# Two partial sums of a convolution block added up later, and a state-space branch that starts each of three parts one step later

## The chip, the cores and the metric

The kernel runs on one core of a Trainium2 chip. Its engines are TensorE (PE, matrix products), VectorE (DVE), ScalarE (ACT) and GpSimd (POOL); each takes its instructions in the order in which the program lists them. GpSimd also issues most of the smaller transfers, SyncE those of the weights. The metric is the device time of one execution in microseconds (us); less is better.

## The reference

Two blocks are computed on 512 tokens of width 1024, in float32. The first is an attention block with a gated feed-forward layer. The second is a mixer of two branches and a mixture of experts. The change is in the mixer, of which this matters:

```python
u = u_a * sigmoid(u_b)                                   # glu
u = silu(layernorm(causal_dwconv(u, cv_dw_w) + cv_dw_b)) # 31 taps per channel
y_cv = u @ w_cv_out
xbc = silu(causal_dwconv(xbc))                           # 4 taps
xs, bm, cm = split(xbc); dt = softplus(...)
y = ssd(xs, dt, a, bm, cm) + d_skip * xs                 # state space, 4 groups
y = rmsnorm_per_group(y * silu(z)); y_ssm = y @ w_ssm_out
return (g_cv * y_cv + g_ssm * y_ssm) @ w_mix_out
```

## The kernel before, in words

Activations lie with channels on the 128 partitions and the 512 tokens along the free axis. Every large product of the mixer is made from three float32r products (high part by high part, and the two mixed ones), `mm3` at L185 to L187. Weights come in through a stream: SyncE loads a raw tile, ACT makes its high part (L80) and DVE its low part (L81), two tiles ahead of their use.

`mixer` runs one list of product stages in a fixed order, `u0 p0 z0 u1 p1 w0 z1 u2 p2 w1 z2 u3 p3 w2 z3 c0 w3`, and then the second half of the gates. A stage `u` makes two blocks of the convolution branch (128 channels each), `p` the inputs of one of four state-space groups, `z` the gates of that group, `w` the group's part of the output product, `c` half of the gates of the convolution branch. Each stage is cut into steps of twelve products of 128x512 and then one call of `tick`; a stage `u`, `z` or `w` has 8 steps, `p` has 12, `c` has 16. Below, u1.7 is the seventh step of stage u1. A tick does not order the work in time by itself: it decides where in each engine's queue the instructions of the side work stand.

Three kinds of side work hang on the ticks:

- `conv31(m, pad, i)`, the 31 taps of block m. Blocks with an even m (`i == 0`) run on DVE, one instruction per tap (L1235). Blocks with an odd m (`i == 1`) are added up by transfers: ACT scales the shifted input into a tile `tap` (L1240), and POOL issues a transfer that adds it to one of two partial sums (L1241), the even taps to `acc`, the odd ones to `two[1]`. After the last tap DVE adds the two sums (L1244), POOL writes the result out to `ucd` (L1245) and adds it to `S1`, the sum over the blocks (L1246). A rate per stage says how many taps go into one tick.
- `ssd(g)`, the state-space group g, a generator that moves one step per tick (every second tick in a stage `w`). Its steps are in order: the products of B and C (L1324), four turns of the inputs (`xtr`, L1339 on PE, L1341 on DVE, L1345 on POOL), the chunk states (`state`, L1352), four pairs of decay matrices (`seg`, L1367 to L1378, their product on DVE at L1372), four outputs (`out`, L1387 and L1391 on PE into one bank psC, emptied by DVE at L1394), a column sum for the norm (L1467 on PE, fed by POOL at L1404), an inverse root on POOL (L144 to L151), diagonal matrices on POOL (L1457), their product (L1461), and the normalized rows `yh`, `yl` (L1449 and L263 on DVE, L262 on ACT). Stage `w` of the group multiplies these rows.
- `ln`, the layer norm of the convolution branch. It waits in its generator until all `conv31` are through, loads the eight blocks again, makes the mean from `S1` (L1530), subtracts it (L1537 on DVE, L1539 on ACT, L1543 on POOL), forms a column sum (L1467 again) and scales.

`WAIT` holds three digits for each group g. `ssd` passes over so many steps before its first products, before its column sum, and (in `rstd_row`) between the inverse root and the diagonal matrices.

After the mixer comes the mixture of experts. Which expert weights it loads is computed from the mixer's output, all but those of its first unit.

Of the kernel before, what the change touches and what calls it, by code (L numbers as in the profile page):

```python
# [13 lines left out]
OP = mybir.AluOpType  # L14
# [1098 lines left out]

WAIT = "000 000 000 000".split()

NTAP = 4  # L1120


def mixer(K, a):
# [6 lines left out]
    v_, s_, p_ = nc.vector, nc.scalar, nc.gpsimd  # L1130
# [89 lines left out]
    ucd = K.dr.tile([8, 128, S], F32, name="ucd")  # L1220
    S1 = g_()
    p_.memset(S1, 0.0)

    def conv31(m, pad, i):
        acc = g_()
        if i == 0:
            v_.tensor_scalar(acc, pad[:, 0:S], K.cw31[:, m, 0:1], K.cols[:, m:m + 1], op0=OP.mult, op1=OP.add)
        else:

            two = (acc, g_())  # L1230
            s_.activation(acc, pad[:, 0:S], AF.Identity, scale=K.cw31[:, m, 0:1], bias=K.cols[:, m:m + 1])
        yield 1
        for k in range(1, 31):
            if i == 0:
                v_.scalar_tensor_tensor(acc, pad[:, k:k + S], K.cw31[:, m, k:k + 1], acc, op0=OP.mult, op1=OP.add)  # L1235
            elif k == 1:
                s_.activation(two[1], pad[:, k:k + S], AF.Copy, scale=K.cw31[:, m, k:k + 1])
            else:
                t = gp.tile([128, S], F32, name="tap", tag="tap", bufs=NTAP)
                s_.activation(t, pad[:, k:k + S], AF.Copy, scale=K.cw31[:, m, k:k + 1])  # L1240
                p_.dma_start(two[k % 2], t, accum_op=OP.add)  # L1241
            yield 1
        if i:
            v_.tensor_tensor(acc, acc, two[1], op=OP.add)  # L1244
        p_.dma_start(ucd[m], acc)  # L1245
        p_.tensor_tensor(S1, S1, acc, op=OP.add)  # L1246

    hold = {}

    def evac_u(q, e, acc):  # L1250
        if e < 2:
            hold[2 * q + e] = acc
            return
        m = 2 * q + e - 2
        th = g_()
        s_.activation(th, acc, AF.Tanh, scale=0.5)
        pad = pad_(30, 4)
        p_.memset(pad[:, 0:30], 0.0)
        v_.scalar_tensor_tensor(pad[:, 30:], th, 1.0, hold.pop(m), op0=OP.add, op1=OP.mult)
        i = m % 2  # L1260
        bg[i].append(conv31(m, pad, i))
# [40 lines left out]
    def pause(n):  # L1302
        for _ in range(n):
            yield

    def ssd(g):
        d = gr[g]
        while not all(i in d for i in range(6)):
            yield
        wait = [int(n) for n in WAIT[g]]  # L1310
        yield from pause(wait[0])
# [207 lines left out]
    def ln():  # L1519
        while bg[0] or bg[1]:  # L1520
            yield
        for m in range(8):
            u = pad_(30, 4) if m < 4 else pad_(3, 3) if m < 7 else gp.tile([128, S], F32, name="tap", tag="tap", bufs=NTAP)
            p_.dma_start(u[:, 0:S], ucd[m])
# [835 lines left out]
def fused_kernel(ctx: ExitStack, tc: tile.TileContext, a, out, dbg=None, stage=9):  # L2360
# [60 lines left out]
    with tc.tile_pool(name="big3", bufs=1) as K.big:  # L2421
        K.ng = 38
        K.taps = {'u': (1.5, 1.5, 1), 'p': (0.1, 0.8, 1), 'z': (2, 1.25, 1), 'w': (1.5, 1, 0.5), 'c': (2.5, 0.25, 1)}
        mixer(K, a)
# [55 lines left out]
```

## Time and profile before

| | |
|---|---|
| time of three runs, median (lowest to highest) | 2449.02 us (2448.45 to 2449.63) |
| the profiled execution: time, span | 2449.14 us, 2447.3 us |
| mean granted TensorE clock, as a share of full speed | 0.986 |
| TensorE busy | 2255.6 us, 92% of the span |
| DVE, ACT, POOL busy | 51%, 33%, 18% of the span |

The span reaches from the first to the last instruction. The mixer's stages lie between about 780 and 1440 us of it. Since matrix products are pipelined, an engine that is busy is not one at its peak; what stands idle before an instruction, and what ended that idle time, is the more telling number.

### The profile page before, as it was taken

How to read it: one execution, taken by the hardware profiler on the slowest of the kernel's cores; microseconds unless marked ns; L12 is line 12 of the kernel's file. 1: busy time of each engine (PE TensorE's matmuls, PEld its weight loads, DVE VectorE, ACT ScalarE, POOL GpSimd, SP SyncE). 2: the span in 40 equal slices, each digit the busy share in tenths (PEclk: the TensorE clock that was granted, in tenths of full speed). 3: DMA queues.
4: the chain of work that ended last, by engine and by line, in shares of the span. 5: the costliest groups of instructions: out<-in, count | busy, mean ns of one | idle time of the engine just before them, and what ended most of it. 6: DMA issues, size and time to landing. Idle time of an engine off the chain costs nothing.

```text
span 2447.3 us, 32777 instructions
## 1 busy us (share of the span) xinstructions
PE 2255.6 (92%) x12323; PEld 1524.1 (62%) x12323; DVE 1259.7 (51%) x2217; ACT 816.9 (33%) x1527; POOL 440.7 (18%) x746
## 2 busy tenths in 40 slices
PE   8999999999999999999999998989889888987775
PEld 6678878878888777787877785434334333433331
DVE  4456656763336677787875646434334334332222
ACT  5455654222225746465653533101001000100002
POOL 2044422230001243334334020000000000000001
PEclk9999999999999999999999999999999999999998
DMA  4121127865323666566653357999999999999996
GB/s 141 54 68 36 53 95 257 277 204 113 101 97 96 153 129 155 125 151 139 158 130 121 109 206 289 426 426 426 427 426 427 426 427 426 427 426 427 427 426 270
DMA packets 197521, 593.28 MB, mean 242 GB/s; under 512 B 16515, under 2 KB 104703, under 8 KB 148720
## 3 DMA queue, kind: packets, MB, share of 16 engines
q1 hardware_dynamic: 168016, 523.94, 55.0%
q0 software_dynamic: 29344, 67.22, 12.4%
q8 instruction: 98, 1.61, 0.2%
q14 instruction: 63, 0.52, 0.1%
HBM read 556.40 MB, written 4.22 MB: 229 GB/s over the span
## 4 chain that ended last, share of the span: by engine, by line
PE 55%; DMA 28%; DVE 8%; ACT 4%; issue 2%; POOL 2%; SPq 0%; ACTq 0%; POOLq 0%; DVEq 0%
DMA we<-in_w_dram 26%; PE psA L185 11%; PE psA L187 11%; PE psA L186 11%; PE psA L2132 3%; PE psA L2148 2%; PE psB L2065 2%; DMA g<-tap 2%; PE psE L185 1%; PE psE L186 1%; PE psE L187 1%; DVE w_l L81 1%; PE psC L765 1%; ACT w_h L80 1%; PE psB L739 1%
## 5 line engine op out<-in xcount | busy, mean ns | idle before, releaser
L81 DVE TENSOR_TENSOR w_l<-w_raw,w_h 128x1024 fp32r<-128x1024 f32 (+1 forms) x224 | 278.3, 1246 | 303.9 <-ACT w_h L80 303.3
L2132 PE MATMUL psA<-we,xe 128*32 128x512 f32 (+1 forms) x2048 | 352.3, 614 | 59.6 <-DMA we<-in_w_dram 58.7
L185 PE MATMUL psA<-xh,w_h 128*128 128x512 f32 (+1 forms) x960 | 379.7, 396 | 0.8 <-ACT w_h L80 0.8
L187 PE MATMUL psA<-xh,w_l 128*128 128x512 f32 (+1 forms) x960 | 368.6, 384 | 0.5 <-DVE w_l L81 0.5
L186 PE MATMUL psA<-xl,w_h 128*128 128x512 f32 (+1 forms) x960 | 368.1, 383 | 0.7 <-DVE xl L263 0.7
L80 ACT CAST w_h<-w_raw 128x1024 fp32r<-128x1024 f32 (+1 forms) x224 | 232.8, 1043 | 236.4 <-PE psA L187 113.7
L2132 PEld LDWEIGHTS psA<-we,xe 128*32 128x32 f32 (+1 forms) x2048 | 88.4, 119 | 275.5 <-issue 169.4
L2148 PE MATMUL psA<-we,t 128*32 128x512 f32 (+1 forms) x1024 | 188.8, 619 | 38.2 <-DMA we<-in_w_dram 37.5
L185 PEld LDWEIGHTS psA<-xh,w_h 128*128 128x128 f32 x960 | 181.4, 189 | 41.1 <-issue 4.9
L186 PEld LDWEIGHTS psA<-xl,w_h 128*128 128x128 f32 x960 | 181.4, 189 | 39.1 <-issue 4.6
L187 PEld LDWEIGHTS psA<-xh,w_l 128*128 128x128 f32 x960 | 181.0, 189 | 37.5 <-DVE w_l L81 1.0
L2114 DVE TENSOR_TENSOR res<-res,psC 128x512 f32<-128x512 f32 x78 | 53.5, 686 | 267.9 <-PE psC L2112 267.8
L2053 POOL TENSOR_TENSOR ow<-ow,owb 128x128 f32<-128x128 f32 x80 | 37.8, 472 | 832.2 <-DVE owb L2052 814.1
L2072 DVE TENSOR_SCALAR xe<-psB,n2c 128x128 f32<-128x128 f32 x76 | 31.0, 408 | 266.1 <-PE psB L2065 266.1
L2065 PEld LDWEIGHTS psB<-o,z 128*128 128x128 f32 x1216 | 143.2, 192 | 34.5 <-issue 23.1
L2065 PE MATMUL psB<-o,z 128*128 128x128 f32 x1216 | 152.4, 278 | 0.3 <-DVE xe L2072 0.3
L1241 POOL DMA_DIRECT2D g<-tap x116 | 101.5, 888 | 245.8 <-ACT tap L1240 175.8
L2148 PEld LDWEIGHTS psA<-we,t 128*32 128x32 f32 (+1 forms) x1024 | 46.6, 119 | 149.8 <-issue 74.2
L2070 ACT ACTIVATE xe<-psB,n2c 128x128 f32<-128x128 f32 x76 | 34.8, 458 | 302.9 <-PE psB L2065 302.9
L2095 ACT COPY t<-psB 128x512 f32<-128x512 f32 x20 | 11.7, 586 | 332.9 <-PE psB L2094 332.9
L185 PE MATMUL psA<-w_h,xh 128*128 128x512 f32 x256 | 104.1, 406 | 1.5 <-DVE xl L399 1.5
L187 PE MATMUL psA<-w_h,xl 128*128 128x512 f32 x256 | 100.1, 391 | 0.0
(656 smaller groups left out, 3913.7 us busy)
## 6 DMA issues: line engine op xcount, KB each, us to landing
we<-in_w_dram SPq DMA_DIRECT2D x380, 1024.0 KB, 19.5
w_raw<-in_w_in_dram SPq DMA_DIRECT2D x64, 512.0 KB, 4.1
g<-tap POOLq DMA_DIRECT2D x116, 256.0 KB, 4.2
t<-in_w_ada_dram POOLq DMA_DIRECT2D x48, 512.0 KB, 6.1
w_raw<-in_ffn_w_in_dram SPq DMA_DIRECT2D x44, 512.0 KB, 4.4
w_raw<-in_fox_w_in_dram SPq DMA_DIRECT2D x32, 512.0 KB, 3.9
w_raw<-in_ffn_w_out_dram SPq DMA_DIRECT2D x27, 512.0 KB, 3.2
w_raw<-in_w_ssm_out_dram SPq DMA_DIRECT2D x16, 512.0 KB, 3.5
```

Source lines behind the costliest of these rows:

```text
L80: nc.scalar.copy(h[:, k], r[:, k])
L81: nc.vector.tensor_tensor(l[:, k], r[:, k], h[:, k], op=OP.subtract)
L185: mm(out, w[0], x[0], start=first, stop=False)
L186: mm(out, w[0], x[1], start=False, stop=False)
L187: mm(out, w[1], x[0], start=False, stop=last)
L1241: p_.dma_start(two[k % 2], t, accum_op=OP.add)
L2053: p_.tensor_tensor(ow[:, t], ow[:, t], b, op=OP.add)
L2065: mm(b, K.Z[:, k, t * 128:(t + 1) * 128], o[:, t], start=t == 0, stop=t == NT - 1)
L2070: s_.activation(x[:, k], b, AF.Identity, scale=A2[:, k:k + 1], bias=B2[:, k:k + 1])
L2114: v_.tensor_tensor(r, r, b, op=OP.add)
L2132: mm(b[r], x[:, 4 * h + k, r], w[e][:, k], start=h == 0 and k == 0, stop=h == 1 and k == 3)
L2148: mm(bs[f][r], hT[:, 2 * h + k, r], w[e][:, k, f * 512:(f + 1) * 512], start=h == 0 and k == 0, stop=h == 1 and k == 1)
```

## The change

The odd convolution blocks 1, 3 and 5 no longer add up their two sums behind their last tap. Their last three instructions (L1244 to L1246) are put into a closure, which the next odd block calls behind its tap number 4. Block 7 and the even blocks end as before. Besides, each of the three pauses of each state-space group is one step long and no longer zero.

```diff
-WAIT = "000 000 000 000".split()
+WAIT = "111 111 111 111".split()
 
 NTAP = 4
+LAND = 4
...
+    ends = []
+
     def conv31(m, pad, i):
         acc = g_()
...
                 p_.dma_start(two[k % 2], t, accum_op=OP.add)
+                if k == LAND and ends:
+                    ends.pop()()
             yield 1
-        if i:
-            v_.tensor_tensor(acc, acc, two[1], op=OP.add)
-        p_.dma_start(ucd[m], acc)
-        p_.tensor_tensor(S1, S1, acc, op=OP.add)
+
+        def end():
+            if i:
+                v_.tensor_tensor(acc, acc, two[1], op=OP.add)
+            p_.dma_start(ucd[m], acc)
+            p_.tensor_tensor(S1, S1, acc, op=OP.add)
+        if i and m < 7:
+
+            ends.append(end)
+            return
+        end()
```

## Rows read from the trace of the kernel before

**Rows 1.** The page: TensorE's line, and the chain of waits by line

```profile
PE 2255.6 (92%) x12323; PEld 1524.1 (62%) x12323; DVE 1259.7 (51%) x2217; ACT 816.9 (33%) x1527; POOL 440.7 (18%) x746
...
DMA we<-in_w_dram 26%; PE psA L185 11%; PE psA L187 11%; PE psA L186 11%; PE psA L2132 3%; PE psA L2148 2%; PE psB L2065 2%; DMA g<-tap 2%; PE psE L185 1%; PE psE L186 1%; PE psE L187 1%; DVE w_l L81 1%; PE psC L765 1%; ACT w_h L80 1%; PE psB L739 1%
```

**Rows 2.** Busy time by stretch of 20 us, 740 to 1440 us

```profile
core 0: us, PE busy (x) PEld busy (x) DVE busy (x) ACT busy (x) POOL busy (x), PEclk, DMA share, GB/s
...
980.00:1000.00 20.00, 20.00 (x101) 15.37 (x100) 19.22 (x26) 11.27 (x27) 8.09 (x9) 1.00 0.77 165
...
1020.00:1040.00 20.00, 15.32 (x74) 12.52 (x73) 12.32 (x15) 3.24 (x4) 5.48 (x5) 0.83 0.29 79
...
sum 700.00, PE 675.08 PEld 544.83 DVE 498.70 ACT 372.39 POOL 219.98; mean PE 19.29 PEld 15.57 DVE 14.25 ACT 10.64 POOL 6.29
```

**Rows 3.** Whom TensorE waited for, 760 to 1440 us: total, times, longest

```profile
PE psC L1387 <- DVE g L1394: 9.1, 3, 4.7
PE psC L1461 <- POOL g L1457: 3.1, 3, 1.7
PE psB L1324 <- DVE g L1289: 3.1, 3, 1.2
PE psC L1530 <- POOL g L1246: 1.9, 1, 1.9
...
PE psE L1467 <- POOL g L1543: 0.6, 1, 0.6
```

**Rows 4.** The line L1244: what it waited for (us, times)

```profile
  DMA g<-tap: 15.2, 3
```

**Rows 5.** TensorE in order of time: start, us, idle before

```profile
859.20 1.55 PE L1352 MATMUL psE<-g 128*128 128x512 f32 x2 [1.84 <-POOL g L1345]
...
911.13 1.98 PE L1387 MATMUL psC<-g 128*64 128x128 f32 x16 [3.20 <-DVE g L1394]
...
921.42 1.05 PE L1467 MATMUL psE<-ones,g 128*128 128x1 f32 x8 [1.35 <-POOL g L1404]
...
932.50 1.13 PE L1461 MATMUL psC<-g,ones 128*128 128x512 f32 x2 [1.74 <-POOL g L1457]
...
1027.47 1.97 PE L1387 MATMUL psC<-g 128*64 128x128 f32 x16 [4.68 <-DVE g L1394]
...
1150.95 1.09 PE L1387 MATMUL psC<-g 128*64 128x128 f32 x16 [1.17 <-DVE g L1394]
```

**Rows 6.** VectorE in order of time

```profile
905.70 0.69 DVE L1244 TENSOR_TENSOR g<-g 128x512 f32<-128x512 f32 x1 [1.93 <-DMA g<-tap]
...
910.34 0.73 DVE L1394 SCALAR_TENSOR_TENSOR g<-g,dsk,psC 128x512 f32<-128x512 f32 x1
...
911.57 1.44 DVE L1397 TENSOR_TENSOR g<-g 128x384 f32<-128x384 f32 x1
...
1022.20 0.69 DVE L1244 TENSOR_TENSOR g<-g 128x512 f32<-128x512 f32 x1 [6.60 <-DMA g<-tap]
...
1099.33 0.68 DVE L1341 TENSOR_TENSOR g<-psB,dt 128x512 f32<-128x512 f32 x1
...
1298.73 0.68 DVE L1244 TENSOR_TENSOR g<-g 128x512 f32<-128x512 f32 x1
...
1306.83 0.69 DVE L1537 TENSOR_TENSOR pad<-pad,g 128x512 f32<-128x512 f32 x1 [6.10 <-DMA pad<-ucd]
```

**Rows 7.** Windows with the granted clock, columns as in rows 2

```profile
911.00:916.00 5.00, 4.87 (x29) 4.28 (x30) 3.30 (x5) 2.19 (x3) 2.85 (x3) 0.66 0.14 52
1027.40:1035.40 8.00, 7.93 (x36) 6.66 (x37) 5.11 (x9) 2.20 (x3) 2.57 (x2) 0.60 0.21 66
```

**Rows 8.** GpSimd in order of time

```profile
1100.16 1.89 POOL L1345 TENSOR_TENSOR g<-g,dec 128x512 f32<-128x512 f32 x1 [3.31 <-DVE g L1341]
...
1284.47 3.40 POOL L1457 TENSOR_SCALAR g<-ident,tiny 128x128 f32<-128x128 f32 x4
```

**Rows 9.** Transfers of the taps: count, KB each, median us to landing

```profile
g<-tap POOLq DMA_DIRECT2D x116, 256.0 KB, 4.2
```

## The prediction

> **What bounds the kernel now.** I read the page first. TensorE is busy for 92% of the span, and in the chain of waits the transfers of the odd convolution blocks (`g<-tap`) hold 2%, some 50 us, a large part for work off to the side [rows 1]. The busy time by stretch comes next: over 700 us around the mixer TensorE works 675.08 us, so at most some 25 us of idle time can be won there; the worst stretch is 1020 to 1040 us, with 15.32 us of work and a granted clock of 0.83. DVE is at 19.22 of 20 us in another stretch, but at 71% over the whole [rows 2]. The waits of TensorE name the places: 9.1 us for DVE to empty psC (L1394), 3.1 us for the diagonal matrices (L1457), 3.1 us for the last input of a state-space group (L1289), 1.9 us for `S1`, and smaller ones [rows 3]. In order of time the three psC waits are 3.20, 4.68 and 1.17 us [rows 5]. VectorE's own row says why DVE is late: L1244, the addition of the two sums, waited three times for a tap's transfer to land, 15.2 us in all [rows 4], and everything behind it in DVE's queue waited too. So the mixer is bound by TensorE, whose idle time comes from DVE's queue and from short hand-overs.
>
> **The deferred sums.** Nothing is taken out: three times L1244, L1245 and L1246 move from behind tap 30 to behind tap 4 of the next odd block. By the rates this is u1.7 to p1.5, u2.2 to p2.4 and u3.2 to p3.4, five steps or more later, while a tap lands in 4.2 us [rows 9]; L1244 then waits for no transfer. What each stall cost:
>
> Block 1: DVE idled 1.93 us and worked 0.69 us on L1244 [rows 6]. Without both, L1394 begins 2.6 us earlier than 910.34, so 0.6 of TensorE's 3.20 us stay [rows 5]. After the wait the clock was 0.66 over 5 us [rows 7], at the 1.2 GHz level for part of it: 5 x 0.34 = 1.7 us lost. Gain 2.6 + 1.7 = 4.3 us.
>
> Block 3: DVE idled 6.60 us [rows 6], more than TensorE's 4.68 us [rows 5]; the wait goes, and with it 8 x 0.40 = 3.2 us of low clock [rows 7]. Gain 7.9 us.
>
> Block 5: 15.2 - 1.93 - 6.60 = 6.7 us of stall [rows 4, 6] reached TensorE as 1.17 us [rows 5], with no low clock after it. Gain 1.2 us.
>
> Together 13.4 us. The stall is not late again elsewhere: what came next for psC were the decay products (L1372), which wait for ACT, and they were ready before L1244 ended.
>
> A rule speaks for smaller stalls. The row has 4.2 us from issue to landing for 256 KB [rows 9]. The Trainium skill, DMA: Bandwidth & Descriptors, Anatomy of one DMA, gives a GpSimd transfer 2.0 us and its bytes at 436 GB/s, by which I estimate 2.6 us; each stall would be 1.6 us shorter, and the gain 13.4 - 4.8 = 8.6 us at the worst. The trace disagrees, and I go by it.
>
> In the new places DVE (0.69 us) and POOL (some 2 us) do the same work beside others. Queued behind it on POOL are taps, and in p1.5 the inverse root of group 0; that is charged below. GpSimd's sum also slows DVE: beside it L1397 took 1.44 us for 384 columns, where L1394 takes 0.73 for 512 [rows 6]. Three such slow-downs are between 0 and 3 us; I take 0, because stages p leave DVE idle and no psC wait stands there.
>
> A rule makes more of this. The Trainium skill, SBUF — State Buffer, Who interferes with whom, says that a DVE instruction with two inputs in SBUF and a GpSimd instruction reading it share a port. By it I estimate no more than the three sums' whole length, about 4 us, lost; the row of L1397 agrees that there is such a slow-down.
>
> **The pauses.** From L1467 at 921.42 to L1461 at 932.50 lie three steps: (932.50 - 1.74 - 921.42 - 1.05) / 3 = 2.76 us for a step of products [rows 5]. One pause lets TensorE do that much more before it asks.
>
> The start of a group: the three waits for L1289, 3.1 us [rows 3], are shorter than a step and go. But the first state product (L1352) has its own chain: DVE's turn L1341, POOL's L1345, TensorE. In group 0 it comes one tick after the turn, and TensorE waits 1.84 us [rows 5]. In groups 1 to 3 it came two ticks after, in stage w; one step later it falls on z.1, one tick after. In group 2 the chain was 1099.33 to 1100.16 + 1.89, or 2.7 us [rows 6, 8], against about 3.3 us that a tick with a turn gives; DVE is late by up to 2 us there. Group 0 keeps 1.84 us; groups 1 to 3 each get between 0 and 1.84 us. I take 0.6, nearer the lower end, because DVE enters z1 to z3 with less work behind it than z0. Gain 3.1 - 1.8 = 1.3 us.
>
> Before the column sum: 1.35 us in group 0 [rows 5] go, under one step.
>
> Before the diagonals: L1461 waits 3.1 us in groups 0, 2 and 3 [rows 3]. In group 0 (1.74 us) the column sum now stands in p1.5 behind the deferred sum of block 1, so POOL starts its root some 2 us later while the step gives 2.76 us: between 0 and 1.74 us gained, I take 0.9. Group 2's 0.2 us go. Group 3 belongs to the next point.
>
> The end. The group's rows are finished three steps later, p1.9 instead of p1.6, and c0.12 instead of c0.9. I counted the ticks of all stages: each group is still done before its stage w, so no step is without products. In c0 this removes the 1.2 us at L1461 and the 1.9 us before L1530 [rows 3], since block 7's L1244 (1298.73) no longer stands behind group 3's rows. But the layer norm now does. L1461 would end near 1296 (1284.47 + 3.40 + 1.1 + three steps, less its wait); its rows take DVE and ACT 8.5 us (1289.0 to 1298.73 with one weight split of 1.2) [rows 6, 8]; after one more split the first L1537 starts about 1306, against 1306.83 now [rows 6]. From there to L1467 DVE and ACT set the pace, as TensorE already waits for L1543 at the end [rows 3]. So of 3.7 us only 0.9 stay, and a wait of 3 us there may lower the clock. I take 0.2, between -0.6 and 3.7.
>
> **The sum.** 13.4 + 1.3 + 1.35 + 0.9 + 0.2 + 0.2 = 17.4 us off the profiled execution's 2449.14 us: 2431.8 us. The median of the runs is 0.12 us lower, so it is the same for both: 2432.
>
> **The rivals.**
>
> *DVE becomes the bound.* With 19.22 of 20 us in stretches of z and u [rows 2] DVE may not run ahead once its stalls are gone. Half of the 13.4 us would stay as waits for L1394, and all first states would cost 1.84 us: 6.7 + 3.1 - 5.5 + 2.65 = 7 us, 2442. Against it: DVE had 6.60 us to spare when it stalled [rows 6]. Chance 0.22.
>
> *The gain is given back.* The expert weights hold 26% of the chain [rows 1]; were their stream set by something that the mixer does not move, the time would stay at 2449. Against it: all but the first unit's addresses come out of the mixer's result. Chance 0.09.
>
> *Slower: the first states wait for transfers.* POOL's L1345 stands behind tap transfers, which themselves wait until the one before last on their sum has landed. One tick after the turn, each group could wait 4.2 us [rows 9] and then run at half clock, 3.2 us at the worst [rows 7]: 4 x 7.4 = 29.6 us where I count 3.6, so 2432 + 26 = 2458. It decides from (17.4 + 3.6) / 4 = 5.2 us for each group. Against it: in group 2 POOL waited for DVE's L1341 [rows 8], not for a transfer. Chance 0.09.
>
> **The numbers.** My forecast has 0.60. By the bounds above it lies between 2425 (no new waits, all of 3.7 us) and 2438 (full waits at the first states, GpSimd's slow-down). A difference of 0.2%, 4.9 us, is about what a measurement tells from none. Faster by more than that: 0.60 + 0.22 = 0.82; within it 0.09; slower 0.09. The range takes the first rival in: 2424 to 2446.
>
> **What would show it.** L1244 of blocks 1, 3 and 5 without a wait for a transfer, and the psC waits of 9.1 us under 1 us; a granted clock of 1.00 around u1.8 and u2.4; no wait of L1324; L1352 waiting in groups 1 to 3 for under 1 us; L1467 of the layer norm waiting 2 to 3 us instead of 0.6. I am wrong if L1394 is still late without L1244 in front of it, or if L1352 waits over 2 us in each group.

## The result, and the profile after

| | before | changed |
|---|---|---|
| median of six runs each | 2448.84 us | 2465.63 us |
| lowest to highest | 2448.45 to 2450.75 us | 2461.45 to 2467.22 us |
| ratio, 95% interval | | 1.0065 (1.0055 to 1.0076) |
| profiled execution: time, span | 2449.14, 2447.3 us | 2465.67, 2463.8 us |
| mean granted clock | 0.986 | 0.979 |

The change makes the kernel slower by 0.65%, 16.8 us. I had forecast 2432 us with a range up to 2446, and gave "slower" one chance in eleven. The forecast was wrong by sign.

Line numbers of the changed kernel are 1 to 12 higher than those of before: L1243 and L1244 are the old L1240 and L1241 (a tap and its transfer), L1251 to L1253 the old L1244 to L1246 (the addition of the two sums and what follows it), L1288 the old L1276 (the memset with which the evacuation of a stage p begins), L1293 the old L1281, L1301 the old L1289, L1336 the old L1324, L1357 the old L1345, L1364 the old L1352, L1406 the old L1394, L1416 the old L1404, L1461 the old L1449, L1469 the old L1457, L1473 the old L1461, L1479 the old L1467, L1485 the old L1473, L1542 the old L1530, L1555 the old L1543.

The deferral did what it should. VectorE's group of the four additions of two sums, by line in the changed kernel (busy us, mean ns, idle before):

```profile
L1251 DVE TENSOR_TENSOR g<-g 128x512 f32<-128x512 f32 x4 | 2.8, 706 | 0.0
```

The 15.2 us of waiting [rows 4] are gone. So are TensorE's waits for psC behind them; but in the list of those that TensorE has now, other names stand first (total, times, longest, 760 to 1440 us, to be held against [rows 3]):

```profile
PE psE L1364 <- POOL g L1357: 10.8, 4, 6.1
PE psA L185 <- ACT w_h L80: 9.2, 3, 4.2
PE psC L1473 <- POOL pad L1288: 6.2, 1, 6.2
PE psC L1542 <- DVE g L1461: 4.3, 1, 4.3
...
PE psE L1479 <- POOL g L1555: 0.9, 1, 0.9
```

The wait of 9.1 us for L1394, the 3.1 us for the last inputs, the 1.35 us of group 0's column sum and the 1.9 us for `S1` no longer stand in it. The first three lines have grown from 1.8, 0.8 and 3.1 us. In the fourth, L1542 (old L1530) waited 1.9 us for `S1` before; now it waits 4.3 for the readers of psC. In order of time (start, us, idle before):

```profile
859.50 1.97 PE L1364 MATMUL psE<-g 128*128 128x512 f32 x2 [1.87 <-POOL g L1357]
...
936.72 2.08 PE L1473 MATMUL psC<-g,ones 128*128 128x512 f32 x2 [6.21 <-POOL pad L1288]
...
981.34 2.07 PE L1364 MATMUL psE<-g 128*128 128x512 f32 x2 [6.13 <-POOL g L1357]
...
1317.32 2.05 PE L1542 MATMUL psC<-g,ones 128*128 128x512 f32 x2 [4.32 <-DVE g L1461]
```

The first states (L1364) of groups 1 and 2 wait 6.13 us at 981.34 and 2.36 us at 1113.05; the two waits of 4.2 us for a weight's high part (L80) come at 1070.47 and 1198.58, behind the rows of groups 1 and 2. The durations say something too: L1473 and L1542 take over 2 us where L1461 took 1.13 [rows 5], that is, they run at half clock. The windows behind three of these waits, with the granted clock third from the end:

```profile
981.30:985.40 4.10, 4.06 (x8) 2.54 (x9) 0.54 (x1) 1.21 (x2) 1.81 (x2) 0.50 0.71 128
...
1198.50:1204.00 5.50, 5.38 (x12) 3.79 (x13) 5.41 (x7) 4.57 (x9) 1.97 (x4) 0.50 0.60 144
1317.30:1323.00 5.70, 5.68 (x17) 3.92 (x18) 2.61 (x3) 3.16 (x5) 0.00 (x0) 0.72 0.31 97
```

An account of the whole can be made. I take the stretch from the transposes of `dt` (L1195, old L1194) to the first transposes behind the mixer (L1714, old L1702), and call it the mixer: 807.85 to 1447.82, or 640.0 us, before; 806.90 to 1465.83, or 658.9 us, now. It grew by 19.0 us. TensorE's idle time in it, summed over the rows in order of time, rose from 23.7 to 35.0 us, and the low clock, as 20 us times what each window lacks to 1.00, from 7.0 to 15.4 us: together 19.7 us more. So the loss is waits and low clock, inside the mixer. The sum is a rough one, as a window's low clock counts its idle part too. The whole span grew by 16.5 us only; the 2.5 us by which the profiled execution was shorter outside the mixer were not followed up.

### The profile page after: what moved, and what is told of

Read it like the earlier page. It is cut to its first block, busy times and chain, and to the rows that moved or that the text cites. A ratio compares the mean times of both kernels' runs of the same rounds, so it can differ in the third digit from the quotient of the medians.

```text
span 2463.8 us, 32772 instructions
## 1 busy us (share of the span) xinstructions
PE 2265.4 (92%) x12323; PEld 1527.9 (62%) x12323; DVE 1263.6 (51%) x2217; ACT 817.7 (33%) x1527; POOL 440.9 (18%) x746
## 4 chain that ended last, share of the span: by engine, by line
PE 52%; DMA 30%; DVE 9%; ACT 5%; issue 2%; POOL 2%; SPq 0%; ACTq 0%; DVEq 0%; POOLq 0%
DMA we<-in_w_dram 29%; PE psA L185 11%; PE psA L187 11%; PE psA L186 11%; PE psA L2144 3%; PE psA L2160 2%; PE psB L2077 2%; DVE w_l L81 1%; DVE g L1238 1%; PE psE L185 1%; DMA g<-tap 1%; PE psE L187 1%; PE psE L186 1%; ACT w_h L80 1%; PE psC L765 1%
## 5 line engine op out<-in xcount | busy, mean ns | idle before, releaser
L81 DVE TENSOR_TENSOR w_l<-w_raw,w_h 128x1024 fp32r<-128x1024 f32 (+1 forms) x224 | 277.6, 1243 | 315.4 <-ACT w_h L80 315.2
L80 ACT CAST w_h<-w_raw 128x1024 fp32r<-128x1024 f32 (+1 forms) x224 | 232.9, 1044 | 240.2 <-PE psA L187 113.2
L2160 PE MATMUL psA<-we,t 128*32 128x512 f32 (+1 forms) x1024 | 193.8, 640 | 38.4 <-DMA we<-in_w_dram 37.7
L1244 POOL DMA_DIRECT2D g<-tap x116 | 101.4, 893 | 246.2 <-ACT tap L1243 155.7
```

The source lines that it names most:

```text
L80: nc.scalar.copy(h[:, k], r[:, k])
L81: nc.vector.tensor_tensor(l[:, k], r[:, k], h[:, k], op=OP.subtract)
L2160: mm(bs[f][r], hT[:, 2 * h + k, r], w[e][:, k, f * 512:(f + 1) * 512], start=h == 0 and k == 0, stop=h == 1 and k == 1)
```

## The experiments

Each was timed in five rounds beside the kernel before, whose median was between 2448.76 and 2449.32 us each time, so that medians can be compared across them. "Mixer" is the length of the stretch above in the one profiled execution.

| kernel | median us | ratio to before (95%) | mixer us |
|---|---|---|---|
| e1 deferral, no pauses | 2441.53 | 0.9973 (0.9964 to 0.9982) | 631.4 |
| e2 pauses, no deferral | 2481.09 | 1.0130 (1.0114 to 1.0145) | 675.0 |
| e3 deferral, first pause | 2459.44 | 1.0043 (1.0030 to 1.0057) | 650.2 |
| e4 deferral, second and third pause | 2449.76 | 1.0003 (0.9994 to 1.0012) | 643.3 |
| e5 changed, mean in another bank | 2463.79 | 1.0055 (1.0041 to 1.0068) | 657.3 |
| e6 changed, rows over four ticks | 2465.53 | 1.0065 (1.0051 to 1.0079) | 658.6 |
| e7 changed, first xd on VectorE | 2455.69 | 1.0031 (1.0020 to 1.0042) | 651.6 |
| e8 changed, diagonals before the pause | 2462.01 | 1.0052 (1.0038 to 1.0066) | 654.2 |
| e9 deferral, two starts, first xd on VectorE | 2438.90 | 0.9957 (0.9943 to 0.9970) | 630.2 |
| e10 deferral, first pause but in group 0 | 2454.83 | 1.0027 (1.0017 to 1.0037) | 643.9 |
| e11 changed, rows one step earlier | 2464.89 | 1.0064 (1.0050 to 1.0078) | 652.8 |
| e12 deferral of blocks 3 and 5 alone | 2444.64 | 0.9983 (0.9974 to 0.9992) | 635.0 |
| e13 changed, four places mended | 2451.91 | 1.0010 (1.0001 to 1.0019) | 642.8 |
| e14 as e9, sum behind tap 8, pause in group 0 | 2448.66 | 0.9999 (0.9990 to 1.0008) | 643.4 |
| e15 changed, sum behind tap 8 | 2463.53 | 1.0061 (1.0047 to 1.0075) | 655.1 |

**Which half of the change is it?** (e1, e2)

```diff
 # e1, from the changed kernel
-WAIT = "111 111 111 111".split()
+WAIT = "000 000 000 000".split()
 # e2, from the kernel before
-WAIT = "000 000 000 000".split()
+WAIT = "111 111 111 111".split()
```

> The deferred closures kept, all twelve pauses back at zero. Theory A (the deferral does what it should, the pauses spoil it): the waits of 9.1 us for psC go and nothing new comes, so 10 to 14 us faster than before, 2435 to 2439 us. Rival B (the three instructions in stage p, in front of GpSimd's root and the group's rows, are what is late): slower than before, 2455 us or more, with the waits for L1461's GpSimd work and for L80 still there.

> The kernel before with all twelve pauses at one. Theory A: the late start of the state products, of the rows of groups 1 and 2 and of the layer norm's mean cost some 25 us with their low clock, while the 9.1 us for psC stay or move, so 2465 to 2480 us. Rival B: without the deferred instructions in front of them the late rows and the root cost nothing, so 2445 to 2452 us.

The deferral alone is 7.5 us faster than before, the pauses alone are 32.0 us slower. Theory A has both signs; but the gain is short of its 10 to 14 us, and the time with the pauses alone, 2481.1 us, lies just above its range. Rival B is out. The two aren't independent: with the pauses in place the deferral is worth 2481.1 - 2465.6 = 15.5 us (in e2, which has the old line numbers, TensorE waits 14.5 us at L1375, a product of the decay matrices, until VectorE empties psE; before its additions of two sums VectorE idles 20.1 us, of which 13.1 are put down to a tap's landing).

**Which pause?** (e3, e4, e10; from the changed kernel)

```diff
-WAIT = "111 111 111 111".split()
+WAIT = "100 100 100 100".split()   # e3
+WAIT = "011 011 011 011".split()   # e4
+WAIT = "000 100 100 100".split()   # e10
```

> The deferral with the first pause alone (before a group's first products). Theory A: the first states of groups 1 and 2 wait for GpSimd's product behind tap transfers, about 8 us and a low clock behind them, so 8 to 12 us above the deferral alone, 2445 to 2450 us. Rival C (the first states were late only because GpSimd and ScalarE were still behind from the stall of group 0's diagonal matrices): L1352's line waits under 3 us in all, and the time is within 3 us of the deferral alone.

> The deferral with the second and third pause, the first at zero. Theory A: the rows of groups 1 and 2 stand at p.3 and those of group 3 at c0.11; the two waits for L80 of 4.2 us, the 6.2 us for group 0's diagonal matrices and the 4.3 us before the layer norm's mean shrink but most of them stay, so 2445 to 2455 us. Rival C: it is the sum of all three pauses that brings the rows behind two evacuations of stage p, so two of them cost under 4 us over the deferral alone, 2437 to 2442 us.

> The deferral and the first pause in groups 1 to 3, none in group 0. Theory A (of the 18 us that the first pause costs, some 10 are group 0's: its diagonal matrices come behind the deferred sum of block 1 in GpSimd's queue): the wait of 8.0 us goes, 2447 to 2452 us. Rival (group 0's wait only takes the place of one that comes anyway, such as the first state of group 1): 2456 us or more, with L1364 at 9 us or more.

Against the deferral alone (2441.5) the first pause costs 17.9 us and the other two 8.2; together 26.1, where the three cost 24.1. They nearly add up. I had expected the first pause to cost half of that. TensorE's waits in e3 show why:

```profile
PE psC L1473 <- POOL g L1469: 9.7, 4, 8.0
PE psE L1364 <- POOL g L1357: 9.5, 4, 3.3
PE psC L1542 <- POOL g L1253: 4.7, 1, 4.7
```

The first pause moves everything of its group, the diagonal matrices too, and behind group 3's rows `S1`'s last sum (L1253). The wait of 8.0 us is group 0's. Without a pause there (e10) it falls to 1.7 and the time by 4.6 us, less than half of the 10 that I had put on it: both theories missed, as the three other groups keep 13.3 us, with L1364 at 10.6 us. For e4 theory A's range holds, and Rival C, that two pauses cost under 4 us, does not. But theory A's waits do not hold either: those for L80 fell from 9.2 to 2.0 us and that of L1542 from 4.3 to 1.6, while those of L1473 grew from 6.2 to 10.1. That the time came out in its range is in part luck.

**The four places of the changed kernel, one at a time.** First the places themselves, in the trace of the changed kernel.

*First state of group 1.* GpSimd in order of time:

```profile
972.93 0.87 POOL L1244 DMA_DIRECT2D g<-tap  x1 [5.04 <-DMA g<-tap]
975.21 0.87 POOL L1244 DMA_DIRECT2D g<-tap  x1 [1.41 <-PE psB L1351]
...
977.87 0.87 POOL L1244 DMA_DIRECT2D g<-tap  x1 [1.23 <-DMA g<-tap]
979.13 0.87 POOL L1244 DMA_DIRECT2D g<-tap  x1 [0.40 <-DVE g L1238]
980.07 1.22 POOL L1357 TENSOR_TENSOR g<-g,dec 128x512 f32<-128x512 f32 x1
```

VectorE's turn (L1353) had ended at 973.55. The product that follows it on GpSimd (L1357) came 6.5 us later, behind tap transfers, of which those at 972.93 and 977.87 had themselves been held until an earlier tap landed. TensorE asked at 975.2 and got it at 981.34.

*Diagonal matrices of group 0.* GpSimd again:

```profile
922.90 0.58 POOL L1252 DMA_DIRECT2D ucd<-g  x1 [1.16 <-DVE tiny L1485]
923.49 1.31 POOL L1253 TENSOR_TENSOR g<-g 128x512 f32<-128x512 f32 x1
924.72 0.68 POOL L144 CAST tiny<-tiny 128x4 f32<-128x4 int32 x1
925.49 1.05 POOL L145 TENSOR_SCALAR tiny<-tiny 128x4 int32<-128x4 f32 x1
...
929.70 0.20 POOL L151 TENSOR_TENSOR tiny<-tiny 128x4 f32<-128x4 f32 x1
930.18 0.92 POOL L1244 DMA_DIRECT2D g<-tap  x1 [0.28 <-issue]
930.80 0.42 POOL L1288 MEMSET pad<- 128x3 f32 x1
932.98 0.86 POOL L1244 DMA_DIRECT2D g<-tap  x1 [1.76 <-ACT tap L1243]
933.58 3.08 POOL L1469 TENSOR_SCALAR g<-ident,tiny 128x128 f32<-128x128 f32 x4
```

The root was ready at 929.90, and the third pause put a transfer, the memset of an evacuation and one more transfer, which had to wait for ScalarE's tap, in front of the matrices: 3.7 us. ScalarE was late with that tap because it had itself idled 5.57 us, before L1291, until this memset came behind the whole root. (The list of waits names the memset L1288 because its event came last; what L1473 reads is L1469.)

*Rows of group 1.* ScalarE:

```profile
1061.52 0.62 ACT L262 CAST g<-g 128x512 fp32r<-128x512 f32 x1 [3.04 <-DVE g L1461]
...
1068.34 0.62 ACT L262 CAST g<-g 128x512 fp32r<-128x512 f32 x1 [1.42 <-DVE g L1461]
...
1069.39 1.03 ACT L80 CAST w_h<-w_raw 128x1024 fp32r<-128x1024 f32 x1
```

From 1060.74 to 1069.68 VectorE and ScalarE hand four rows to and fro, and the weight's high part stands behind them; TensorE waited for it at 1070.47. *The layer norm's mean:* VectorE read psC for the last of group 3's rows from 1316.44 to 1317.18; TensorE's L1542, which writes psC, began at 1317.32.

```diff
 # e5: the mean's product
-        b = K.bank("C")
+        b = K.bank("B")
         mm(b, K.ones[:, 0:128], S1, start=True, stop=True)
 # e6: the rows, in ssd
             K.split(yh[m], yl[m], y)
+            if g in (1, 2) and m < 3:
+                yield
 # e7: in xtr
-                p_.tensor_tensor(xd, x, bc8(dec, c), op=OP.mult)
+                (v_ if c == 0 else p_).tensor_tensor(xd, x, bc8(dec, c), op=OP.mult)
 # e8: third pause behind the diagonal matrices (col_row gets the wait)
-        yield from pause(1 + wait)
-        return (yield from col_row(r))
+        yield
+        return (yield from col_row(r, wait))
...
         yield
         yield
+        yield from pause(wait)
         b = K.bank("C")
 # e11
-WAIT = "111 111 111 111".split()
+WAIT = "111 110 110 111".split()
 # e15
-LAND = 4
+LAND = 8
```

> The changed kernel, with the product for the layer norm's mean (L1542) put into a bank of psB instead of the one bank psC. Theory A (psC is held by group 3's rows until the last L1461 has read it): the wait of 4.3 us and the half clock behind it go, so 4 to 6 us below the changed kernel, 2459.5 to 2461.5 us. Rival (it is S1 or DVE itself that is late): the wait stays under another name (L1253) or goes on to L1479 of the layer norm, and the time is within 2 us of the changed kernel's 2465.6.

> The changed kernel, with the four normalized rows of groups 1 and 2 made at four ticks instead of one. Theory A (the two waits of 4.2 us for L80 stand behind the 8 us chain of rows between DVE and ScalarE): both waits fall under 1.5 us and the clock behind them stays up, so 8 to 12 us below the changed kernel, 2454 to 2458 us. Rival (ScalarE is behind there anyway, from the evacuations of p.3 and p.4): the waits stay above 3 us each, and the time is within 3 us of 2465.6.

> The changed kernel, with the first of each group's three products xd (L1357, c = 0) on VectorE instead of GpSimd. Theory A (the first state waits because GpSimd's product stands behind tap transfers): of the 10.8 us of L1364 less than 4 stay and the half clock behind the longest goes, so 7 to 13 us below the changed kernel, 2453 to 2458 us. Rival (VectorE's turn is late itself): L1364 keeps over 7 us, now for VectorE, and the time is within 3 us of 2465.6.

> The changed kernel, with the third pause moved from ahead of the diagonal matrices to behind them, so that GpSimd makes them right behind the root while their product stays at its tick. Theory A (in group 0 they stand behind the memset and the taps of p1.7): the wait of 6.2 us falls to under 3 and the half clock behind it goes, so 4 to 8 us below the changed kernel, 2457.5 to 2461.5 us. Rival (GpSimd's root itself is late, since the deferred sum stands in front of it): the wait stays above 4 us, and the time is within 3 us of 2465.6.

> The changed kernel with the third pause of groups 1 and 2 at zero: their rows come at the third step of stage p instead of the fourth. Theory A (in the fourth they stand behind two evacuations and in front of a weight's split): the waits of L185 for L80 fall from 9.2 us to under 3, so 7 to 11 us below the changed kernel's 2465.6, 2454.5 to 2458.5 us. Rival (those waits only take the place of others a few steps on, as the rows over four ticks left the time where it was): within 3 us of 2465.6.

> The changed kernel, with the deferred sum behind tap 8 (p1.10, p2.9, p3.9) instead of tap 4 (p1.5, p2.4, p3.4), out of the way of group 0's root and of the rows of groups 1 and 2. Theory A (the memset and the taps of p1.7 are in front of the diagonal matrices, and the two evacuations in front of the rows, whether the sum is there or not): the wait for L1473 keeps 4 us or more, and the time is within 4 us of the changed kernel's 2465.6. Rival B (it is the deferred sum in stage p that is late): the 6.2 us and the two 4.2 us go, 2452 us or less.

e7 is clear, the only one of the six whose interval lies apart from the changed kernel's: 9.9 us below it, by moving four short products to an engine that has more to do than GpSimd. Its waits at L1364:

```profile
PE psE L1364 <- POOL g L1357: 3.9, 1, 3.9
PE psE L1364 <- DVE g L1357: 1.1, 1, 1.1
```

The other three of the changed kernel's list stand there untouched, to the same tenth of a microsecond. The wait of 3.9 us is that for group 1's second product, still on GpSimd, and there is half clock behind it: the low clock in the mixer is 15.4 us as in the changed kernel, so what e7 won is idle time alone. Theory A has the time right, and the first product's wait; that under 4 us would stay and the half clock would go is not what came. e8 gained 3.6 us by the medians, a little less than expected: the wait for L1473 fell from 6.2 to 3.0, with half clock still behind it.

e5 took the wait of 4.3 us away altogether, but L1479 of the layer norm went from 0.9 to 2.7 us, and the time fell by 1.8 us, which the two intervals do not separate from nothing. psC was what held the mean, as theory A says; but the time is the rival's, and little of it hung on psC.

The rows taught me most. Over four ticks (e6) the waits for L80 fell from 9.2 to 4.3 us, but now they came in the output stages w1 and w2, with 0.7 us for L81 beside each, and the low clock in the mixer rose from 15.4 to 19 us: time unchanged. One step earlier (e11) they fell to 1.1 us, and this came up instead:

```profile
1051.21 2.01 PE L1473 MATMUL psC<-g,ones 128*128 128x512 f32 x2 [2.77 <-POOL pad L1288]
...
1177.41 1.12 PE L1473 MATMUL psC<-g,ones 128*128 128x512 f32 x2 [1.26 <-POOL g L1469]
```

The median moved by 0.7 us, the mixer of the profiled execution by 6.1; that execution was the shortest of five, so the size stays open and lies between. The rivals' forecast of the time holds in both, and so does the reason of e11's: these waits take each other's place. The reason of e6's rival does not, as no wait there stays above 3 us (the longest is 1.9). e15 keeps theory A: with the deferred sum moved out of the way of the root and of the rows, L1473 still waits 3.9 us (4 were expected), L80 6.6 us, and the time is 2.1 us lower, not clear of noise. The sum's own part is the difference, 2.3 us at L1473 and 2.6 at L80.

**All four together** (e13: the edits of e5, e7, e8 and e11).

> The changed kernel with the four places mended together: the first product xd on VectorE, the diagonal matrices ahead of the third pause, the layer norm's mean in another bank, and the rows of groups 1 and 2 one step earlier (third pause zero there). Theory A (these places are the whole of what the pauses cost): their single gains of 10.4, 4.1, 2.3 and 0.7 us add up, so 2446 to 2450 us, no worse than the kernel before. Rival (pauses cost by themselves, or one wait takes the place of another): 2454 us or more.

It is 13.7 us below the changed kernel, and 10.4 us above the deferral without pauses; it lies between the two expectations. Its waits that are left are of the same kinds (total, times, longest):

```profile
PE psC L1474 <- POOL pad L1288: 5.8, 2, 3.1
PE psE L1364 <- DVE g L1357: 3.4, 3, 1.7
PE psE L1480 <- POOL g L1556: 2.6, 1, 2.6
PE psE L1364 <- POOL g L1357: 2.6, 1, 2.6
```

So the four places are the larger part of the cost of the pauses, not all of it.

**What the deferral was worth, block by block** (e12).

```diff
 # from e1
-        if i and m < 7:
+        if i and 1 < m < 7:
```

> No pauses, and the deferral for blocks 3 and 5 alone; block 1 ends as in the kernel before. Theory A (block 1's stall of 3.2 us and its low clock were only exchanged for the wait of the column sum and a low clock there): within 2.5 us of the deferral alone, 2439 to 2444 us. Rival (block 1 is worth the 4.3 us of the prediction, and it is the others that gave less): 2444.5 us or more.

It came out on the border between the two: block 1's deferral is worth 3.1 us by the medians and 3.6 in the mixer, not far from the prediction's 4.3; blocks 3 and 5 give 4.1 by the medians and 5.0 in the mixer, where the prediction had 9.1. TensorE's waits in e1:

```profile
PE psB L1336 <- DVE g L1301: 5.5, 4, 2.4
PE psE L1479 <- POOL g L1416: 2.0, 1, 2.0
PE psC L1542 <- POOL g L1253: 1.9, 1, 1.9
```

L1336, the first product of a group, waits for the last input 5.5 us instead of 3.1; in group 2 it is 2.42 instead of 0.70, in group 3 0.90 instead of none. TensorE gets there sooner, and VectorE does not. The column sum of group 0 (L1479) waits 2.0 us instead of 1.35; the 1.9 us of L1542 were there before.

**A version from what was learnt** (e9, e14): the deferral, a pause only where TensorE was waiting for something that a step does bring (the last inputs of groups 1 and 2), and the first product off GpSimd's queue.

```diff
-WAIT = "111 111 111 111".split()
+WAIT = "000 100 100 000".split()   # e9, with the edit of e7
+WAIT = "010 100 100 000".split()   # e14, with that edit and LAND = 8
```

> The deferral, the first pause in groups 1 and 2 alone, no other pause, and each group's first product xd on VectorE. Theory A (a pause is worth its wait where GpSimd's queue is not what ends last): against the deferral alone the waits of L1336 in groups 1 and 2 (1.0 and 2.4 us) go and the first states wait under 1.5 us each, so 1 to 5 us below it, 2436 to 2441 us, faster than both kernels. Rival (the later start costs by itself): 2444 us or more.

> The kernel with two starts later and the first product on VectorE, and besides the deferred sum behind tap 8 instead of tap 4 and the second pause of group 0 at one. Theory A (group 0's column sum is asked for one step too early; the sum of block 1 is only harmful in front of its diagonal matrices): the wait of 1.9 us for L1416 and the half clock behind it (3.4 us) go, so 2 to 6 us below that kernel's 2438.9, 2433 to 2437 us. Rival (the wait goes on to the diagonal matrices or to the last inputs, behind the later sum): 2438 us or more.

e9 is 9.9 us faster than before and 26.7 faster than the changed kernel, and within theory A. That it also beats the deferral alone (by 2.6 us) the intervals don't settle. e14 refutes my reading of group 0: the column sum's wait of 1.9 us went, but L1473 waited 6.96 us instead. It moves two things at once, and they were not taken apart: the waits of L1364 in groups 1 and 2 also grew, from 0.90 and 1.39 us in e9 to 3.51 and 2.98, so that group 0 is only part of its 9.8 us. VectorE in group 0:

```profile
917.34 2.33 DVE L1293 SCALAR_TENSOR_TENSOR g<-pad,cw,g 128x512 f32<-128x512 f32 x3 [0.44 <-ACT g L1291]
920.07 2.33 DVE L1293 SCALAR_TENSOR_TENSOR g<-pad,cw,g 128x512 f32<-128x512 f32 x3 [0.41 <-ACT g L1291]
922.31 0.15 DVE L1485 TENSOR_SCALAR tiny<-psE 128x4 f32<-128x4 f32 x1
```

L1485 is the small step between the column sum and GpSimd's root. The column sum was there at 917.2; one tick later in stage p means one more evacuation's three taps in front of it, 2.7 us with their wait. In e1, a step earlier, it began at 919.42, behind one set only. The pause bought TensorE one step of 2.76 us and cost its supplier as much, and then the root's first four instructions took 0.5 to 1.1 us each instead of 0.2 (more on that below).

## Why the prediction was wrong

**The failed step.** It is the sentence on which all terms of the pauses rest: "One pause lets TensorE do that much more before it asks", 2.76 us. That is right for TensorE and wrong for the chain that serves it. A tick later, the group's instructions stand behind one more tick's work in each engine's queue: in stage p an evacuation (VectorE's 2.33 us of L1293, ScalarE's copy and first tap, GpSimd's memset), in stages w and z tap transfers that hold GpSimd (group 1) or taps and additions on VectorE (group 2). I priced what a pause gives and never what it is moved behind. The terms of -1.3 (starts), -1.35 and -0.9 (group 0), -0.2 (group 2) and -0.2 (end), a gain of some 4 us, became a loss of 24.1 (2465.6 - 2441.5). Neither of the two signs by which I would have known that I was wrong appeared: no wait for L1394 (now L1406) was left, and L1352 (now L1364) waited over 2 us in two groups, not in each. No sign was set for the rows and for group 0's diagonal matrices, where another 8.4 and 4.5 us of waiting came up.

**Start of the groups.** L1336 waits no more, as forecast. The first states were to wait 0.6 us in groups 1 to 3, at the most 1.84: they waited 6.13, 2.36 and 0.43. This was the rival "first states wait for transfers", to which I gave 0.09. My evidence against it, that GpSimd waited for VectorE's turn in group 2 [rows 8], was one group of three, with two ticks of room. With one tick GpSimd's queue decided in group 1. In group 2 it was again VectorE: GpSimd idled 1.77 us for its turn L1353, which began at 1110.29 behind taps (L1238) and additions of stage w (L1496), and then took 1.88 us for L1357. So of the 6.13 and 2.36 us only the larger is the rival's mechanism. The rival asked for 5.2 us in each group and got it in one; e7 shows that it was nevertheless the largest place.

**Group 0.** Of the 1.74 us at L1473 I took 0.9 as gained. They became 6.21. I had seen the deferred sum in front of the root (2 us), which is there, but not what the third pause puts between root and matrices.

**Rows of groups 1 and 2.** No term for them at all, and that without a reason. I had counted that they are finished before their stage w, and not looked whose weights stand behind them on ScalarE. It measured two waits of 4.2 us; yet e6 and e11 show that most of them would only have come up elsewhere.

**The end.** I forecast that L1479 of the layer norm would wait 2 to 3 us, since the rows push the subtraction. It waits 0.88; instead L1542 waits 4.32, because psC is one bank and the rows read it. With the mean in another bank (e5) L1479 waits 2.66, as forecast: the chain was right, its first link was missed.

**The deferral.** Right in every sign that I named: no wait for a landing, no psC wait, and in the changed kernel a clock of 1.00 from 900 to 920 and from 1020 to 1040 us. (In e1, the deferral alone, the clock was 0.90 from 900 to 920 us and 0.93 in the 20 us after it, behind the wait of the column sum.) Mis-sized: 13.4 forecast, 7.5 measured (e1). In e1 the stretch from group 1's L1336 (957.25) to group 2's (1078.20) is 120.95 us where it was 127.0 in the kernel before; that is 6.1 won of block 3's 7.9, and the missing 1.7 is L1336's longer wait. From group 2's L1336 to group 3's, where block 5's 1.2 us should have shown, it is 120.92 us where it was 120.04: nothing was won there. My sentence that the stall is not late again elsewhere looked only at what came next for psC. Rival 1, VectorE as the bound, had 2442 us for its sum; its place was wrong (not L1394 but L1301). Its half of the 13.4 us, 6.7, is near what the deferral alone brought; that its 2442 us in all is near e1's 2441.5 is luck, since it has the pauses' terms in it.

**Not settled.** With four places mended, 10.4 us of the pauses' cost remain, in waits of one to three us whose low clock I could not take apart. The low clock and the waits aren't independent, so that gains of single mends need not add up: e5, e7, e8 and e11 gave 16.0 us one by one by the medians, of which only e7's 9.9 are clear of noise, and 13.7 together.

## What to carry to other kernels

In a weave of queues written out by hand, "one step later" gives the consumer a step and puts one more step's work in front of the producers; before adding a pause, list for every link of the chain what that later place in its own queue stands behind, and give slack only where the producer's queue is short there (that the two pauses kept in e9 gained anything by themselves is not shown). When two edits come together, price them apart: here one was worth -7.5 us and the other +24.1. And a wait that is taken away is worth only the distance to the next one, which has to be looked up on all engines, not only on the buffer where the wait was seen.

## What the hardware showed beyond that

The low clock behind a wait did not go by the length of the wait. In the changed kernel, behind the wait of 6.13 us, 4.1 us ran at 0.50 (the 1.2 GHz level) and the next 1.6 at 0.83; behind 4.21 us, 5.5 us at 0.50 and 2.0 at 0.90; behind 6.21 us, 5.3 us at 0.54. In e1, behind 1.98 us, it was 4.6 us at 0.57, 2.0 at 0.50 and 2.0 at 0.79. What these stretches lack to full clock is 2.3, 3.0, 2.4 and 3.4 us: the shortest of these waits was the dearest, at more than its own length again. Behind the waits of 2.36 us in the changed kernel (1113.05) and of 2.42 us in e1 (1078.20) the clock stayed at 1.00.

GpSimd and VectorE slowed each other, in group 0 of the changed kernel as follows. This pair of VectorE instructions took 2.76 us where two such took 1.29 in e14, and the weight's split behind it took its usual time:

```profile
922.59 2.76 DVE L1301 SCALAR_TENSOR_TENSOR g<-g 128x512 f32<-128x512 f32 x2
925.27 1.21 DVE L81 TENSOR_TENSOR w_l<-w_raw,w_h 128x1024 fp32r<-128x1024 f32 x1
```

Beside the pair stood GpSimd's sum L1253, 1.31 us from 923.49. The root's small instructions take 0.19 to 0.20 us; the first two took 0.68 and 1.05, and ended at 925.40 and 926.54, just as the pair (925.35) and the split (926.48) did. In e14 the pair had only such small instructions beside it, and lost nothing. The kernel before has the same loss elsewhere: L1372's pair took 2.84 us beside the sum L1246 (907.30), and 1.28 in block 5, where that sum came later. So the deferral moved this slow-down rather than added it; the 0 that I took for it on VectorE was not shown to be wrong, but I had no term for GpSimd's root.

The Trainium skill, SBUF — State Buffer, Who interferes with whom, says that a VectorE instruction with two inputs in SBUF contends with a GpSimd instruction that reads SBUF. The trace agrees: L1301 and L81 have two such inputs, L1253 and the root's instructions read SBUF, and both sides lost.
